# The context's expert rows in four parts of 64 tokens, rows of v of one part alternating with rows of u of the next

## The chip, the core and the metric

The kernel runs on one core of a Trainium2 chip. The metric is the device time of one launch in microseconds (us). The engines are TensorE (PE, whose weight loads the profile shows apart as PEld), VectorE (DVE), ScalarE (ACT), GpSimd (POOL), and SyncE (SP), which issues the plain loads. Every engine takes its instructions in a fixed order that was settled when the program was built; an instruction whose input is not there holds up all that stands behind it on its engine.

## The reference

Two layers over 256 latent tokens (`x`, 256x1024 float32) and 256 context tokens (`z`). The first layer updates both streams; the last one needs the context only for the scan's state. Per layer and stream:

```python
px = modulate(rmsnorm(x)) @ w_in          # columns: q,k,v | beta | alpha | gate | pool | fourier
x  = x + xg1 * mixer_out(px, scan(px))    # gated DeltaNet in chunks of 64, pooling, 2-D Fourier
hx = modulate(rmsnorm(x))
x  = x + xg2 * peer(hx)

def peer(h):                              # 8 heads, 16 of 128x128 experts each
    q = (h @ w_query).reshape(t, 8, 2, 128)
    s_top, i_top = top_k(q . sub_keys, 16)
    best, pos = top_k(s_top[0][:, None] + s_top[1][None], 16)
    idx, gate = i_top[0] * 128 + i_top[1], softmax(best)      # 128 choices per token
    act = gelu(einsum('td,tkd->tk', h, expert_u[idx]))
    return einsum('tk,tkd->td', gate * act, expert_v[idx])
```

A row of `expert_u` or `expert_v` is 1024 float32, 4 KB. A token needs 128 rows of each.

## The kernel before, in words

The program is written stage by stage for layer 0: the context's columns (the input projection with its convolutions), its scan and its update; the *context select* (`gather_select`: the choice of the 128 experts of each context token); then the latent columns, scan and update; the *latent select* (`dense_select`); `build`, which writes a dense table of gates to memory; and `stream`, which runs over all 128 slices of the expert tables for the latent tokens. Layer 1 follows in the same manner without a context select. A scheduler then moves instructions of later stages forward where their inputs and their buffers allow it, and fixes one order for each engine. So stages overlap, and what a stage may overlap with is set by engines, PSUM banks and SBUF space.

The latent tokens go through all experts (`stream`): in each of 128 iterations a slice of u and one of v (512 KB each) is loaded (L1100), split into a high part (ACT, L1106) and a low one (DVE, L1107), multiplied with the tokens (24 matmuls on PE, L1117 to L1119, into PSUM bank `s`), put through gelu (ACT, L1121), weighted (DVE, L1132, L1135; ACT, L1133) and multiplied with the slice of v (12 matmuls, L1140).

The context tokens fetch just their rows, by indirect DMAs of 128 rows that POOL issues (L970, `gather_rows`). Before the change the two halves of 128 tokens go by two ways.

- Tokens 0 to 127, *by choice*. For each of the 128 choices one gather brings a row of u for each token (`uv<-in_u`, 128x1024, 512 KB), and DVE multiplies it with the tokens and sums (L982, below "a dot"). Then, token by token, one gather brings the 128 rows of v that a token has chosen (`uv<-in_v`), and PE sums them with the weights (L1005; four matmuls for a pair of tokens, into bank `s`). There are seven buffers `uv`. All 256 of these gathers are written ahead of the stream (`EARLY = 256`), and the sums share bank `s` with the stream's scores.
- Tokens 128 to 255, *by token*. For each choice one gather brings u and v side by side (`uv<-in_uv`, 128x2048, 1 MB, from a table that holds both), DVE makes the dot (L1021), ACT gelu and gate (L1024, L1025), and DVE adds the weighted v to a sum (L1029). These 128 gathers are written inside the stream, ahead of the context's work for layer 1 (`context`), which needs their result.

In the context select DVE carries the searches for the largest scores (L772 to L780), the pairs (L825 to L866) and the index (L938); `oh` (L232) is a step of it on POOL, and the query projection (`po<-hT,w`, L256) runs on PE. In the latent columns `pj<-hT,w` and `pj<-w,hT` (L256) are the projections, `xpad` the padded input of the convolution, L495 and L497 the convolution on DVE. L632 opens the latent scan, whose steps `C` (L232) are on POOL, the queue of the gathers. L324 opens a normalization: that of `t` the columns, that of `xn` the latent select.

Of the kernel before, what the change touches and what calls it, by code (L numbers as in the profile page):

```python
# [95 lines left out]
def _layout(i):  # L96
# [25 lines left out]
    for l in range(depth):  # L122
# [9 lines left out]
        if l < depth - 1:  # L132
            a[f"u{l}"], a[f"v{l}"] = i["expert_u"][l], i["expert_v"][l]
            a[f"uv{l}"] = np.concatenate([i["expert_u"][l], i["expert_v"][l]], 1)
# [11 lines left out]
def _body(st, tc, a, out, dbg, until):  # L146
# [761 lines left out]

    def gather_select(l, s, m, rows, done):

        idx = rows("idx", [128, NB, HEADS * TOPK], 1, I32)
        idx_t = rows("idx_t", [128, T], 1, I32)
        gate = rows("gate", [128, NB, HEADS, TOPK])
        st = {}
        sc, sh = scales(l, 1, m, s)
        h2 = [normed(X[s, b], rows(f"h2{b}", [128, D]), f"n{b}") for b in range(NB)]
        done()
        sp = Stage("select")
        with using(c0="po", c1="po"):
            hT = transposed(h2, sc, sh, sp("hT", [128, KT, T]))  # L920

        def by_token():
            for b in range(NB):
                for half in range(2):
                    p = bank([128, 4, 128], f"c{half}")
                    for k in range(4):
                        pe.transpose(p[:, k], hT[:, half * 4 + k, b * 128 : b * 128 + 128], ident)
                    act.copy(h2[b][:, half * 512 : half * 512 + 512], p.rearrange("p a b -> p (a b)"))
# [5 lines left out]
        def after(h):  # L934
            if h == 0:
                by_token()
            for t in (idx, idx_f):
                dve.scalar_tensor_tensor(  # L938
                    t[:, :, h * TOPK : h * TOPK + TOPK], keys[0][:, :, 0], float(NKEYS), keys[0][:, :, 1],
                    op0=OP.mult, op1=OP.add,  # L940
                )

        keys = [None]
        idx_f = sp("idx_f", [128, NB, HEADS * TOPK])
        select(l, sp, (hT,), pair, lambda h, n: gate[:, :, h : h + n], GROUPS, after)

        p = bank([128, T], "c2")
        for b in range(NB):
            pe.transpose(p[:, b * 128 : b * 128 + 128], idx_f[:, b], ident)
        dve.tensor_copy(idx_t, p)  # L950
        for b in range(NB):
            st["h2", b], st["idx", b], st["gate", b] = h2[b], idx[:, b], gate[:, b]
            dump(f"idx{l}{s}{b}", st["idx", b])
            dump(f"gate{l}{s}{b}", st["gate", b])
        st["idx_t"] = idx_t
# [334 lines left out]
```

## Time and profile before

| what | us |
|---|---|
| median of three runs (3271.42 to 3287.86) | 3277.94 |
| the profiled execution, its own time | 3268.07 |
| its span, first to last instruction | 3266.3 |
| PE busy | 2874.7 (88%) |
| DVE busy | 2211.1 (68%) |
| ACT busy | 1349.3 (41%) |
| POOL busy | 860.3 (26%) |

What lies outside the span is 1.8 us. Busy shares are means over stages with different limits, so the table alone doesn't tell what a stage waits for; the rows further down are taken stage by stage. The gathers are the software queue in the profile: 268.46 MB of 746.52 MB in all.

### The profile page before, as it was taken

To read this page: it belongs to the slowest core of one execution; us is meant where nothing else is said; L and a number is where in the kernel's file an instruction comes from. 1 tells how busy PE (TensorE), PEld (TensorE's weight loads), DVE (VectorE), ACT (ScalarE), POOL (GpSimd) and SP (SyncE) were. 2 spreads that over 40 slices of the span, in tenths; PEclk is the share of its full clock that TensorE was granted. 3 is DMA by queue.
4 is the path that set the end of the run, shared out by engine and by line. 5 is a ranking of instruction groups with operands and counts; after the bars stand their busy time and mean duration, and the time that the engine had idled before them with its cause. 6 is when DMAs were issued, how large, how long until landed. Compare 5 with 4: busy or idle time off the path is not lost. (4 is left out here: it accounts for less than half of the span.)

```text
span 3266.3 us, 47152 instructions
## 1 busy us (share of the span) xinstructions
PE 2874.7 (88%) x17467; PEld 2362.5 (72%) x17467; DVE 2211.1 (68%) x4920; ACT 1349.3 (41%) x2352; POOL 860.3 (26%) x638
## 2 busy tenths in 40 slices
PE   7998985779796887887899999999779889999998
PEld 4686845637351776776778999867678778889997
DVE  4534979777880888898885655742599865555555
ACT  4432232101350444444455645542335644544443
POOL 0150148973545333333310123133320000000000
PEclk9998987779999999999899999999889999999999
DMA  7631466697999999999976543361335576666663
GB/s 260 207 103 54 138 244 194 201 330 254 354 373 351 375 369 365 362 395 387 360 278 197 161 140 118 94 221 43 100 123 176 205 237 202 200 210 202 213 212 130
DMA packets 246165, 746.52 MB, mean 229 GB/s; under 512 B 21168, under 2 KB 94256, under 8 KB 225456
## 3 DMA queue, kind: packets, MB, share of 16 engines
q1 hardware_dynamic: 190320, 474.54, 43.3%
q0 software_dynamic: 55296, 268.46, 22.1%
q8 instruction: 137, 2.24, 0.3%
q14 instruction: 92, 0.75, 0.1%
q10 hardware_dynamic: 320, 0.52, 0.1%
HBM read 707.27 MB, written 35.65 MB: 227 GB/s over the span
## 5 line engine op out<-in xcount | busy, mean ns | idle before, releaser
L1117 PE MATMUL s<-Hh,hu 128*128 128x256 f32 x2048 | 605.5, 296 | 75.7 <-ACT hu L1106 53.6
L1119 PE MATMUL s<-Hh,lu 128*128 128x256 f32 x2048 | 603.9, 295 | 55.5 <-DVE lu L1107 55.4
L1118 PE MATMUL s<-Hl,hu 128*128 128x256 f32 x2048 | 596.1, 291 | 0.0
L1117 PEld LDWEIGHTS s<-Hh,hu 128*128 128x128 f32 x2048 | 408.4, 199 | 100.8 <-ACT hu L1106 63.6
L1107 DVE TENSOR_TENSOR lu<-w,hu 128x1024 fp32r<-128x1024 f32 x256 | 317.0, 1238 | 225.4 <-ACT hu L1106 224.7
L1119 PEld LDWEIGHTS s<-Hh,lu 128*128 128x128 f32 x2048 | 408.8, 200 | 68.7 <-DVE lu L1107 68.6
L1107 DVE TENSOR_TENSOR lv<-w,hv 128x1024 fp32r<-128x1024 f32 x256 | 314.4, 1228 | 181.2 <-ACT hv L1106 168.1
L1118 PEld LDWEIGHTS s<-Hl,hu 128*128 128x128 f32 x2048 | 409.0, 200 | 7.8
L1106 ACT CAST hu<-w 128x1024 fp32r<-128x1024 f32 x256 | 267.8, 1046 | 328.3 <-PE s L1118 252.6
L1106 ACT CAST hv<-w 128x1024 fp32r<-128x1024 f32 x256 | 267.4, 1045 | 161.3 <-PE pj L1140 117.8
L970 POOL DMA_INDIRECT uv<-in_uv,idx x128 | 208.4, 1628 | 404.6 <-DVE acc L1029 383.4
L982 DVE SCALAR_TENSOR_TENSOR uv<-uv,h 128x1024 f32<-128x1024 f32 x128 | 193.4, 1528 | 38.7 <-DMA uv<-in_u,idx 37.8
L232 POOL TENSOR_TENSOR C<-L,levels 128x512 f32<-128x512 f32 x96 | 136.8, 1436 | 292.6 <-DMA g<-gd 161.1
L970 POOL DMA_INDIRECT uv<-in_u,idx x128 | 174.5, 1364 | 44.7 <-issue 25.2
L1140 PE MATMUL po<-hv,wh 128*128 128x512 f32 x512 | 164.9, 402 | 13.2 <-ACT wh L1133 12.2
L970 POOL DMA_INDIRECT uv<-in_v,idx_t x128 | 132.3, 1034 | 122.2 <-PE s L1005 95.2
L1140 PE MATMUL po<-lv,wh 128*128 128x512 f32 x512 | 162.4, 398 | 0.6 <-DVE lv L1107 0.5
L1029 DVE SCALAR_TENSOR_TENSOR acc<-uv,dot,acc 128x1024 f32<-128x1024 f32 x127 | 162.6, 1281 | 0.0
L1140 PE MATMUL pj<-hv,wh 128*128 128x512 f32 x512 | 162.5, 397 | 0.0
L1133 ACT CAST wh<-we 128x256 fp32r<-128x256 f32 x256 | 103.4, 404 | 143.0 <-DVE we L1132 78.3
L1088 PEld LDWEIGHTS c<-one,two 128*128 128x128 f32 x1024 | 123.6, 193 | 53.3 <-issue 33.2
L1140 PE MATMUL po<-hv,wl 128*128 128x512 f32 x512 | 161.8, 397 | 0.0
(427 smaller groups left out, 6007.5 us busy)
## 6 DMA issues: line engine op xcount, KB each, us to landing
w<-in_tab SPq DMA_DIRECT2D x512, 512.0 KB, 4.7
w<-in_wmod SPq DMA_DIRECT2D x96, 512.0 KB, 4.8
gd<-gs SPq DMA_DIRECT2D x32, 1024.0 KB, 5.3
g<-gd SPq DMA_DIRECT2D x32, 1024.0 KB, 8.5
w<-in_wq SPq DMA_DIRECT2D x48, 512.0 KB, 4.2
w<-in_win SPq DMA_DIRECT2D x44, 512.0 KB, 4.3
w<-in_wrest SPq DMA_DIRECT2D x24, 512.0 KB, 3.7
w<-in_wout SPq DMA_DIRECT2D x24, 512.0 KB, 5.3
```

The source lines that it names most:

```text
L232: pool.tensor_tensor(out, x, y, op=op)
L970: pool.indirect_dma_start(out=t, out_offset=None, in_=a[f"{table}{l}"], in_offset=bass.IndirectOffsetOnAxis(ap=index, axis=0))
L982: dve.scalar_tensor_tensor(u, u, 1.0, st["h2", b], op0=OP.mult, op1=OP.mult, accum_out=dots[:, j : j + 1])
L1029: dve.scalar_tensor_tensor(acc, uv[:, D:], dot, acc, op0=OP.mult, op1=OP.add)
L1088: pe.matmul(p[:, t], two[:, t], one[:, t], start=True, stop=True)
L1106: act.copy(hi, raw)
L1107: eng(lo, raw, hi.bitcast(F32), op=OP.subtract)
L1117: pe.matmul(p, hi[:, ks], Hh[:, k], start=(k == 0), stop=False)
L1118: pe.matmul(p, hi[:, ks], Hl[:, k], start=False, stop=False)
L1119: pe.matmul(p, lo[:, ks], Hh[:, k], start=False, stop=(k == KT - 1))
L1133: act.copy(wh, w)
L1140: pe.matmul(acc[b][n], x[:, ts], y[:, n * 512 : n * 512 + 512], start=(i == 0 and j == 0), stop=(i == NKEYS - 1 and j == 2),)
```

## The change

All 256 context tokens now go by choice, in four parts of 64 tokens. A gather of u holds two choices of the 64 tokens of a part (the lower half of the partitions one choice, the upper half the next), so a part needs 64 gathers of u, and 64 gathers of v, one for each token. `sums(i)`, the rows of v of part i, alternates with `scores(i + 1)`, the rows of u of the next part, one gather of each in turn. The table with u and v side by side and the way by token are gone, and with them L1024, L1025 and L1029. In all there are 512 gathers of 512 KB, where there were 256 of 512 KB and 128 of 1 MB: the same number of bytes.

The select now makes an index in the new layout for each head as soon as it is known: two small DVE instructions, eight small matmuls into bank `s`, a DVE copy. It also makes a copy of the tokens for each part (16 matmuls, two ACT copies) and takes the gates' softmax for all heads at the end. The buffers of the gathers (`uv`, `wz`, `h2`) now live in the stage `rows`, which is open from the context select on; before, `uv` and `wz` were opened after it. The sums of parts 0 and 1 use bank `s`, those of parts 2 and 3 bank `c2`. All gathers are written ahead of the stream.

```diff
-        h2 = [normed(X[s, b], rows(f"h2{b}", [128, D]), f"n{b}") for b in range(NB)]
+        h2 = [rows(f"h2{i}", [128, D]) for i in range(PARTS)]
...
         def after(h):
-            if h == 0:
-                by_token()
-            for t in (idx, idx_f):
-                dve.scalar_tensor_tensor(
...
+            if h < PARTS:
+                by_token(h)
+            js = slice(h * TOPK // 2, (h + 1) * TOPK // 2)
...
+                    pe.matmul(
+                        p[c * FEW : c * FEW + FEW, i], ident[:, o : o + FEW], idx_f[:, i * FEW // 128, c, js],
+                        start=True, stop=True,
+                    )
+            dve.tensor_copy(idx[:, :, js], p)
...
+        def scores(i):
+            dots = rows("dots", [128, FEW], 2)
+            for j in range(FEW):
+                u = fetch("u", st["idx"][:, i, j : j + 1])
+                dve.scalar_tensor_tensor(u, u, 1.0, st["h2"][i], op0=OP.mult, op1=OP.mult, accum_out=dots[:, j : j + 1])
+                yield
...
+        def sums(i):
+            dve.tensor_copy(spots_of, w_t[i].rearrange("p (g r) -> p g r", g=2))
+            p = bank([128, 512], VB[i])
+            for r in range(pairs):
+                vs = []
+                for g in range(2):
+                    t = i * FEW + g * pairs + r
+                    vs.append(fetch("v", st["idx_t"][:, t : t + 1]))
+                    yield
...
+        yield from scores(0)
+        for i in range(PARTS):
+            chains = [sums(i)] + ([scores(i + 1)] if i + 1 < PARTS else [])
+            while chains:
+                for c in list(chains):
+                    if next(c, c) is c:
+                        chains.remove(c)
+                    else:
                         yield
...
-    ROWS, EARLY = 7, 256
+    ROWS = 7
+    VB = ("s", "s", "c2", "c2")
...
-    fetching = gather_rows(0, CTX, m, rows, chosen)
-    for _ in range(EARLY):
-        next(fetching)
...
+    for _ in gather_rows(0, CTX, m, rows, chosen):
+        pass
```

The scheduler's order after the change differs in many places. Three of them follow; a number behind a name only tells buffers of one name apart.

On POOL, around the context select, before: the padding of the latent columns (`xpad`) stands ahead of the select's `oh`, and no gather stands between the `oh`.

```order
L232 TENSOR_TENSOR S_1992<-S_407_1946,dc_357 128x512
L482 MEMSET xpad_783_3490 128x2x2
L483 MEMSET xpad_783_3490 128x2x2
L482 MEMSET xpad_784_3491 128x2x2
L483 MEMSET xpad_784_3491 128x2x2
L232 TENSOR_TENSOR oh_2675<-oh_2675,tif_2626 128x1024
L232 TENSOR_TENSOR oh_2803<-oh_2803,tif_2754 128x1024
L232 TENSOR_TENSOR oh_2901<-oh_2901,tif_2852 128x1024
```

The same engine and place after: two `oh`, then 16 gathers of u, two `oh`, and so on; 55 gathers stand ahead of `xpad`, of which the last and the first two behind it are here.

```order
L984 DMA uv_7077<-in_u,idx_2452 128x1024
L481 MEMSET xpad_798_3624 128x2x2
L482 MEMSET xpad_798_3624 128x2x2
L481 MEMSET xpad_799_3625 128x2x2
L482 MEMSET xpad_799_3625 128x2x2
L984 DMA uv_7080<-in_u,idx_2452 128x1024
L984 DMA uv_7083<-in_u,idx_2452 128x1024
```

The latent columns have moved from ahead of the context select to behind it. Counted over POOL's order, ahead of the latent scan's `qd` (L232) there are 104 gathers after and 25 before; ahead of `Hl` (L232), in the latent select, 201 and 141; ahead of the last `oh` of the latent select 231 and 161.

On DVE, inside the context select, before: convolutions of the latent columns (L497) among the searches.

```order
L778 MAX best_2528<-rest_654_2965 128x8
L497 SCALAR_TENSOR_TENSOR y_3647<-xpad_783_3490,convw,y_3647 128x256
L780 MAX_INDEX pos_2963<-best_2528,rest_653_2964 128x8
L778 MAX tv_2949<-rest_646_2951 128x8
L857 TENSOR_TENSOR oh_2901<-ij_2896,places 128x1024
```

The same engine and stage after: dots (L993) among the searches.

```order
L993 SCALAR_TENSOR_TENSOR uv_6942,dots_6914<-uv_6942,h_526_2455 128x1024
L844 TENSOR_SCALAR start_2924<-row_2921 128x32
L849 CAST ij_2929<-row_2921 128x2x16
L777 MAX tv_2878<-rest_624_2880 128x8
L777 MAX tv_2878<-rest_625_2881 128x8
L993 SCALAR_TENSOR_TENSOR uv_6945,dots_6914<-uv_6945,h_526_2455 128x1024
L777 MAX tv_2878<-rest_626_2882 128x8
```

Between the first search and the copy of `idx_t` there are 48 convolution steps (L495, L497) and no dot before, and 48 dots and no convolution after. Up to the first instruction of the latent scan DVE has 15 dots before and 79 after; up to the stream 128 and 192.

On PE, inside the stream, before: the second products of an iteration (L1140) are followed by the first products of another (L1117).

```order
L1140 MATMUL po_7691<-hv_8440,wl_8447 128x512
L1140 MATMUL pj_1843_7692<-hv_8440,wl_8447 128x512
L1140 MATMUL pj_1844_7693<-hv_8440,wl_8447 128x512
L1117 MATMUL s_7694<-Hh_4947,hu_7857 128x256
L1118 MATMUL s_7694<-Hl_4948,hu_7857 128x256
```

The same after, where matmuls on rows of v (L1016) stand between them.

```order
L1138 MATMUL pj_2135_8786<-hv_9534,wl_9541 128x512
L1138 MATMUL pj_2136_8787<-hv_9534,wl_9541 128x512
L1016 MATMUL c_1926_8036<-uv_8085,wz_6912 32x512
L1016 MATMUL c_1926_8036<-uv_8080,wz_6912 32x512
L1016 MATMUL c_1926_8036<-uv_8085,wz_6912 32x512
L1115 MATMUL s_8788<-Hh_5081,hu_8951 128x256
L1116 MATMUL s_8788<-Hl_5082,hu_8951 128x256
```

Parts 2 and 3, 64 pairs of tokens or 256 such matmuls, stand inside the first 62 iterations of the stream, with 64 dots on DVE beside them. The 256 matmuls of parts 0 and 1 stand ahead of the stream, the first 100 of them ahead of the end of the latent scan.

## Rows read from the trace of the kernel before

**Rows 1.** Windows: busy (count) of PE, PEld, DVE, ACT, POOL; clock, DMA share, GB/s.
```profile
320.00:441.00 121.00, 111.42 (x531) 91.61 (x530) 112.20 (x611) 32.92 (x79) 17.58 (x9) 0.99 0.43 129
441.00:486.00 45.00, 39.57 (x152) 24.37 (x150) 29.27 (x65) 10.99 (x28) 28.70 (x25) 0.84 0.88 331
486.00:736.00 250.00, 173.79 (x865) 127.14 (x865) 209.89 (x307) 45.91 (x107) 214.01 (x157) 0.76 0.73 243
736.00:866.00 130.00, 111.11 (x596) 72.31 (x596) 108.01 (x584) 27.47 (x47) 53.27 (x43) 0.96 0.81 286
866.00:1052.00 186.00, 156.61 (x879) 72.66 (x880) 96.94 (x284) 63.85 (x67) 90.66 (x87) 0.98 0.98 372
1052.00:1673.00 621.00, 514.88 (x2933) 447.19 (x2931) 542.32 (x709) 271.02 (x582) 208.45 (x128) 0.93 0.97 368
1673.00:2045.00 372.00, 370.64 (x2450) 335.67 (x2451) 219.25 (x335) 206.21 (x324) 59.29 (x47) 1.00 0.50 162
```

**Rows 2.** Timelines, landmarks: start us, us, engine line op names [idle before].
```profile
319.94 0.87 DVE L772 MAX8 tv<-sco 128x8 f32<-128x128 f32 x4 [3.56 <-ACT sco L805]
...
763.65 0.87 DVE L772 MAX8 tv<-sco 128x8 f32<-128x128 f32 x4 [14.55 <-ACT sco L805]
...
848.58 0.22 DVE L866 TENSOR_TENSOR sel<-oh 128x64 f32<-128x64 bf16 x1
```

**Rows 3.** DVE in the context select: groups (count, busy us, mean ns, idle before), first row.
```profile
L497 DVE SCALAR_TENSOR_TENSOR y<-xpad,convw,y 128x256 f32<-128x256 f32 x36 | 15.9, 478 | 0.0
```

**Rows 4.** Two lines over the whole trace: ns min/median/max, first and last start.
```profile
L324 ACT ACTIVATE t<-x x6: 1039/1056/1059, 6.3 to 2047.7; 128x1024 f32<-128x1024 f32 x6
L324 ACT ACTIVATE h<-x x2: 1039/1048/1057, 293.2 to 295.3; 128x1024 f32<-128x1024 f32 x2
...
L632 DVE TENSOR_TENSOR L<-c,mask_l x10: 676/684/692, 142.6 to 2166.2; 128x512 f32<-128x512 f32 x10
```

**Rows 5.** DVE between 486 and 736 us, groups; the dots.
```profile
L982 DVE SCALAR_TENSOR_TENSOR uv<-uv,h 128x1024 f32<-128x1024 f32 x109 | 170.4, 1581 | 30.9 <-DMA uv<-in_u,idx 30.1
```

**Rows 6.** POOL between 486 and 736 us, groups.
```profile
L970 POOL DMA_INDIRECT uv<-in_u,idx x104 | 147.6, 1420 | 29.0 <-issue 20.8 <-DVE uv L982 5.0 <-PE c L667 0.6
L232 POOL TENSOR_TENSOR C<-L,levels 128x512 f32<-128x512 f32 x24 | 32.2, 1348 | 0.4
```

**Rows 7.** POOL in the latent scan, timeline.
```profile
564.55 1.78 POOL L970 DMA_INDIRECT uv<-in_u,idx  x1 [0.16 <-issue]
566.63 0.94 POOL L970 DMA_INDIRECT uv<-in_u,idx  x1 [0.30 <-DVE uv L982]
```

**Rows 8.** Instructions on `uv` over the whole trace: ns min/median/max, first and last start.
```profile
L970 POOL DMA_INDIRECT uv<-in_v,idx_t x128: 932/938/2458, 722.8 to 1042.6; - x128
```

**Rows 9.** Waits between 980 and 1060 us: us in total, times, longest.
```profile
PEld s L1005 <- DMA uv<-in_v,idx_t: 63.6, 45, 2.8
DVE upd L904 <- DMA h<-sum: 63.0, 1, 63.0
```

**Rows 10.** Matmuls on rows of v, window: busy us (records) of PE and PEld.
```profile
950.00:1000.00 50.00, 26.48 (x112) 3.64 (x106) 0.97 1.00 377
```

**Rows 11.** Stream beside the gathers, 1052 to 1673 us, groups.
```profile
L970 POOL DMA_INDIRECT uv<-in_uv,idx x128 | 208.4, 1628 | 404.6 <-DVE acc L1029 383.4 <-DVE upd L904 10.7 <-DVE uv L1021 5.7
...
L1021 DVE SCALAR_TENSOR_TENSOR uv<-uv,h 128x1024 f32<-128x1024 f32 x128 | 156.3, 1221 | 5.3 <-DMA uv<-in_uv,idx 5.3
...
L1107 DVE TENSOR_TENSOR lu<-w,hu 128x1024 fp32r<-128x1024 f32 x81 | 99.1, 1224 | 51.3 <-ACT hu L1106 51.3
```

**Rows 12.** Rest of that stream, 1673 to 2045 us, groups, first row.
```profile
L1117 PE MATMUL s<-Hh,hu 128*128 128x256 f32 x367 | 107.7, 293 | 0.6 <-ACT we L1121 0.6
```

**Rows 13.** Layer 1's stream, 2900 to 3200 us, groups.
```profile
L1107 DVE TENSOR_TENSOR lu<-w,hu 128x1024 fp32r<-128x1024 f32 x53 | 65.0, 1226 | 62.9 <-ACT hu L1106 62.9
```

**Rows 14.** The fastest 50 us of DMA in the stream.
```profile
1450.00:1500.00 50.00, 41.50 (x244) 35.94 (x243) 45.58 (x60) 22.14 (x49) 18.27 (x11) 0.93 1.02 398
```

**Rows 15.** DMA issues: count, KB each, us to landing.
```profile
w<-in_tab SPq DMA_DIRECT2D x512, 512.0 KB, 4.7
```

More of the change, by code (lines that the diff above doesn't have):

```diff
@@ L947, in gather_select @@
-        p = bank([128, T], "c2")
+        idx_f = sp("idx_f", [128, NB, 2, HEADS * TOPK // 2])
+        gate = sp("gate", [128, NB, HEADS, TOPK])
+        select(l, sp, (hT,), pair, lambda h, n: gate[:, :, h : h + n], (HEADS,), after)
+        gate_c = sp("gate_c", [128, NB, 2, HEADS * TOPK // 2])
         for b in range(NB):
[L949 to L954, printed above, removed]
@@ L1033, in gather_rows @@
-        make = Stage("by_choice")
-        yield from by_choice(make, 0)
-        make.close()
-        make = Stage("by_token")
-        acc = yield from by_token(make, 1)
-        make.close()
-        halves = [[t[:, n * 512 : n * 512 + 512] for n in range(2)] for t in (st["h2", 0], acc)]
-        residual(l, s, m, halves)
+        def scores(i):
[4 more added lines that the diff above has]
+                yield
+            p = bank([128, FEW], VB[i])
+            for c in range(2):
+                cs = slice(c * FEW, c * FEW + FEW)
+                pe.matmul(p[cs], dots, ident[:, cs], start=True, stop=True)
+            w = w_t[i] = rows("w_t", [128, FEW], 2)
+            act.activation(w, p, AF.Gelu)
+            dve.tensor_tensor(w, w, st["gate_t"][:, i * FEW : i * FEW + FEW], OP.mult)
@@ new lines, in sums @@
+        def sums(i):
[7 more added lines that the diff above has]
+                    yield
+                for n in range(2):
+                    for g in range(2):
+                        o = 32 * (2 * n + g)
+                        pe.matmul(
+                            p[o : o + 32], wz[:, g * pairs + r], vs[g][:, n * 512 : n * 512 + 512],
+                            start=(r == 0), stop=(r == pairs - 1), tile_position=(0, o),
+                        )
+            out = rows("uv", [128, D], ROWS)[:, 0:512]
+            act.copy(out, p)
+            b, o = divmod(i * FEW, 128)
+            for n in range(2):
+                act.dma_start(
+                    st["h2"][2 * b][o : o + FEW, n * 512 : n * 512 + 512], out[n * FEW : n * FEW + FEW]
+                )
@@ L1206, in _body @@
         modulation(1, (1, 0))
+    for _ in gather_rows(0, CTX, m, rows, chosen):
+        pass
     def context():
-        for _ in fetching:
-            pass
         rows.close()
```

115 lines of the change are left out of this document (38 added, 77 removed).

## The prediction

> **What bounds the kernel now.** I read the stages in windows first [rows 1], then the landmarks that part them [rows 2, 4], then each stage's groups and waits. The windows show four kinds of stage. In the context select (320 to 441 us) DVE is busy 112.2 of 121 us, PE 111.4, and POOL hardly at all; 48 convolution steps of the latent columns run inside it, 36 of them L497 [rows 3], so that only 45 us lie between its end and the first instruction of the latent scan at 486. In the latent scan and update (486 to 736) POOL is busy 214 us and idle between gathers for another 29 [rows 6]: gathers and the scan's steps `C` take turns on one queue [rows 7], and this queue sets the pace, though DVE has 210 us of work too. In the latent select (736 to 866) DVE leads with 108 of 130. From 866 to 1052 the DMA queues are full (0.98, 372 GB/s). At the end of it DVE stands still for 63 us before the residual's first update [rows 9], because the stream can start only when the sums have left bank `s`.
>
> The stream then has two parts. Beside the wide gathers (1052 to 1673) it makes 81 iterations [rows 11] in 621 us, 7.67 us each, with DVE at 542 us and the DMA queues at 0.97. After them PE is busy 370.6 of 372 us. An iteration that PE alone bounds takes 300 / 53 = 5.66 us [rows 13]. The rest of that stretch has 367 / 8 = 46 iterations [rows 12], 260 us, so the context's work for layer 1 costs PE some 110 us of it.
>
> **The change part by part.**
>
> A. *The context select.* Eight heads of a select that carries neither gathers' dots nor another stage's convolutions take 848.8 - 763.7 = 85 us [rows 2]. The 48 dots that the order puts into the context select come on top, on the engine that leads. A dot takes 1.22 us by itself [rows 11] and 1.58 + 0.08 beside POOL's issuing [rows 5]; I take 1.5, since gathers are issued beside these too: 72 us. The index copies, eight short ones, add 2. From 320 that makes 479 instead of 441: +38. With 1.22 the end is 464; with 1.66 and a wait for the landing of 30.1 / 109 = 0.28 us for each [rows 5] it is about 498.
>
> B. *The latent columns.* Today they are hidden behind the select but for 45 us. In the new order their normalization, transposes, projections and convolutions all stand behind the copy of `idx_t`; the buffers of the gathers are now held from the select on, and I take that to be the reason, which no row shows. Their whole length is paid. The nearest stages are layer 1's latent columns, 2166.2 - 2047.7 = 118 us from normalization to scan, and the context's, 142.6 - 6.3 = 136 us [rows 4]. Both split their operands and need three products where the layer 0 latent columns need one, but have no dots beside them, where this stage has 31. I take 112, close to the nearer one, with 95 and 136 as the ends. The scan then starts at 479 + 112 = 591 instead of 486: **+105**, between 464 + 95 - 486 = +73 and 498 + 136 - 486 = +148. This is the term on which the forecast rests.
>
> C. *Latent scan and update.* Between `qd` and `Hl` POOL issues 201 - 104 = 97 gathers instead of 141 - 25 = 116. With 1.42 us and 29.0 / 111 = 0.26 idle for each [rows 6], 19 fewer are worth 19 x 1.68 = 32 us. DVE has 59 dots here instead of 113, so it leaves the pace to POOL for certain; and a gather's issue takes between 0.93 and 1.78 us [rows 7, 8], the short one where no dot runs, so the rest gets cheaper as well. On the other side 25 pairs of rows of v now stand in PE's order among the steps of the scan, and each can wait for its landing. I take **-40**. At best all gathers take 0.94 + 0.26 and the other 58 us of POOL's work stay (214 less 147.6 for u and 8 for v): 97 x 1.20 + 58 = 174 instead of 250, -76; a context scan and update without gathers took 293.2 - 142.6 = 151 us [rows 4], so that isn't out of reach. At worst the waits on v eat most of the gain: -10.
>
> D. *Latent select.* Thirty gathers instead of twenty stand ahead of its last `oh`, with some ten dots on the leading engine: 10 x 1.3 = 13 us, part of it in the 14.6 us that DVE waits for the first scores [rows 2]. I take **+8** (0 to +25).
>
> E. *From there to the stream.* Gathers up to the last row of part 1: 320 - 231 = 89, instead of 95. The stretch is bound by them and by the DMA queues, so it stays near 186 us; fewer pairs of v on PE (22 instead of some 43) free buffers sooner. I take **-5**. If the gathers were no bound, DVE's 96.9 us [rows 1] and 46 dots at 1.3 would be: 157 us, -29; at worst +5.
>
> F. *The stream of layer 0.* What goes: 128 dots, 128 weighted sums and the small gelus in lockstep with them, two instructions of 1.2 to 1.3 us in each step on DVE. What comes: 64 dots on DVE, and 64 pairs of rows of v on PE. A pair costs 26.48 us for 112 records, eight to a pair: 1.9 us [rows 10]; with a little waiting I take 2.0. The 62 iterations that carry them need 62 x 5.66 + 64 x 2.0 = 479 us of PE. DMA needs for the same 192 gathers of 0.524 MB and 62 iterations of two loads of 512 KB [rows 15] and 0.13 MB of gates, 174 MB, which at the 368 GB/s of the stretch before [rows 1] is 473 us. Two resources that both need all of the time don't overlap perfectly; I take 495. The other 66 iterations at 5.66 and the context's 110 give 484. Together 979 against 621 + 372 = 993, -14; the residual's four updates now stand only two iterations behind the last sum, which may cost DVE, and the low halves `lu` behind it, 4. So **-10**. At best DMA runs at 398 GB/s [rows 14] and the matmuls of a pair hide half their time: about -50. At worst PE waits for each pair as it did ahead of the stream, 63.6 us in 45 waits [rows 9]: 64 waits of 1.4 are 90, less what the buffers cover, +35.
>
> *On the size of the gathers.* The wide gathers, 1 MB each, run with the loads at 368 GB/s, and the 512 KB ones with 377 [rows 1, 10]: no loss for the smaller size shows. The Trainium skill (DMA: Bandwidth & Descriptors, section "Measured (HBM→SBUF, 128 partitions, SWDGE, issued from GpSimd)") advises to batch transfers to 1 MiB or more, and the section on the anatomy of a DMA gives some 2.0 us of fixed cost for each; by that, as an estimate, 192 gathers at 3.2 us in a row would need 614 us and make the stream 120 us longer. This trace disagrees, since gathers overlap, and F stands as it is.
>
> G. *The rest*, layer 1, isn't touched. The latent columns of layer 1 wait for the end of the stream, so a shift there goes to the end in full.
>
> The sum: +105 - 40 + 8 - 5 - 10 = +58. The profiled execution took 3268.07 us (its span and 1.8 us around it), so 3326 by that execution; the median of the runs shown is 9.9 us above it, and I state 3335.
>
> **The rivals.**
>
> 1. *The gathers were the brake, and fewer of them per stage give the shift back.* C and E at their best with the rest as forecast: 105 - 76 + 8 - 29 - 10 = -2, 3276, no change. For it: POOL's 1.78 against 0.94 us. Against: both need that every wait for a row of v is hidden, in stages whose order puts PE and POOL in turn.
>
> 2. *The other side: the stream gains as well.* Its mechanism is the lockstep between DVE's dots, ACT's gelus and the low halves `lu` at 7.67 us an iteration: with the wide dots gone, PE alone sets the pace. It is priced at F's best, -50, and with rival 1 gives -42, 3236. With the rest as forecast it makes the kernel faster by more than 16 us once the scan starts less than 71 us late (71 - 40 + 8 - 5 - 50 = -16); at 105 late it needs rival 1 as well. For it: DVE's 542 of 621 us. Against: PE gets 128 us of new work just there, and DMA's need is the same.
>
> 3. *PE pays for the rows of v.* All of C's gain is lost and F is at its worst: 105 - 10 + 8 + 35 = +138, 3416. For it: PE waited in 45 places for 63.6 us ahead of the stream. Against: there the DMA queues were full, in the scan they are at 0.73.
>
> 4. *The overlap isn't lost.* If the latent columns start earlier than their place in the order makes it seem, B shrinks to the 45 us it costs today, the scan starts 38 us late and the sum is -9, 3269. Against: an engine doesn't pass over an instruction, and on DVE, PE and POOL alike the columns stand behind the select.
>
> **How the numbers follow.** The forecast has 0.65, rival 1 0.12, rival 2 0.07, rival 3 0.13, rival 4 0.03. The forecast's own range is 3295 to 3380. Two in ten may be left out: 3270 to 3400 leaves rival 2 and the far end of rival 3. About 0.5%, 16 us, is what a measurement of this kernel can tell from no change. Slower than that: the forecast almost whole and rival 3, 0.77; no change: rivals 1 and 4 in the main, 0.13; faster: rival 2 and a part of rival 1, 0.10.
>
> **What would show it.** A and B: the last search of the context select ends between 464 and 498 us, the first L631 comes near 591, and no convolution starts before the select's end. C: POOL's gathers between `qd` and `Hl` average under 1.42 us, and L324 of the latent select comes some 65 us later than 736. E and F: the first matmul of the stream near 1110, 62 iterations of about 8 us with PE busier than now, then 5.7 us. Wrong it would be if the convolutions ran inside the select, or if the scan took under 180 us, or if the stream's first 62 iterations came near 7 us.

## The result, and where the time went

The changed kernel takes 3407.31 us, the median of 4 runs (3403.23 to 3412.97), beside 3274.68 us for the kernel before (median of 4). The ratio is 1.0404, with a 95% interval of 1.0361 to 1.0447: 4% slower, above the forecast of 3335 us and 7 us above its range of 3270 to 3400. The direction was as forecast. Of the mechanism, the lost cover of the latent columns was; the largest single loss, 64 more gathers ahead of the stream, was not. The shift between the two profiled spans is 3402.5 - 3266.3 = 136.2 us, where the sum had 58.

The windows of the changed kernel, from landmark to landmark (columns as in [rows 1]; the edges are the landmarks of the table below):

```profile
312.20:478.00 165.80, 83.43 (x519) 68.41 (x518) 145.65 (x617) 15.66 (x34) 72.80 (x56) 0.73 0.57 197
478.00:621.00 143.00, 119.58 (x516) 73.63 (x516) 78.74 (x218) 35.20 (x86) 64.82 (x60) 0.89 0.80 280
621.00:841.00 220.00, 189.17 (x1054) 112.11 (x1054) 119.25 (x181) 44.78 (x107) 163.41 (x136) 0.93 0.71 235
841.00:978.80 137.80, 98.72 (x483) 65.40 (x480) 120.73 (x576) 22.07 (x41) 63.35 (x48) 0.85 0.81 281
978.80:1177.90 199.10, 141.70 (x714) 77.05 (x714) 164.57 (x421) 71.99 (x72) 106.26 (x93) 0.84 0.97 352
1177.90:1685.60 507.70, 503.45 (x2780) 339.62 (x2781) 270.58 (x382) 170.01 (x256) 218.24 (x189) 0.99 0.94 338
1685.60:2177.60 492.00, 489.88 (x3226) 442.23 (x3225) 283.72 (x413) 255.59 (x398) 61.41 (x46) 1.00 0.54 168
```

The same windows with the gathers alone (us, POOL busy and count, clock, DMA share, GB/s):

```profile
312.20:478.00 165.80, 57.42 (x48) 0.73 0.57 197
478.00:621.00 143.00, 62.24 (x55) 0.89 0.80 280
621.00:841.00 220.00, 107.00 (x90) 0.93 0.71 235
841.00:978.80 137.80, 43.31 (x39) 0.85 0.81 281
978.80:1177.90 199.10, 106.26 (x93) 0.84 0.97 352
1177.90:1685.60 507.70, 218.24 (x189) 0.99 0.94 338
```

The landmarks in the changed kernel (one line each: ns min/median/max, first and last start, as in [rows 4]); `pair` ends the context select, `sel` the latent one:

```profile
L865 DVE TENSOR_TENSOR pair<-oh x8: 205/220/225, 328.5 to 478.0; 128x64 f32<-128x64 bf16 x8
L865 DVE TENSOR_TENSOR sel<-oh x8: 200/211/227, 922.3 to 978.8; 128x64 f32<-128x64 bf16 x8
```

```profile
L631 DVE TENSOR_TENSOR L<-c,mask_l x2: 682/687/692, 621.0 to 624.6; 128x512 f32<-128x512 f32 x2
```

```profile
L323 ACT ACTIVATE xn<-x x2: 1055/1056/1058, 841.0 to 842.5; 128x1024 f32<-128x1024 f32 x2
```

```profile
L1115 PE MATMUL s<-Hh,hu x2048: 277/283/583, 1177.9 to 3380.4; 128*128 128x256 f32 x187
```

```profile
L903 DVE TENSOR_TENSOR upd<-po,row x2: 692/692/692, 2177.6 to 2180.7; 128x512 f32<-128x512 f32 x2
```

The same landmarks in the kernel before:

```profile
L866 DVE TENSOR_TENSOR pair<-oh x8: 211/220/224, 333.5 to 440.0; 128x64 f32<-128x64 bf16 x8
L632 DVE TENSOR_TENSOR L<-c,mask_l x2: 680/686/691, 486.2 to 492.6; 128x512 f32<-128x512 f32 x2
L324 ACT ACTIVATE xn<-x x2: 1056/1056/1057, 736.5 to 737.9; 128x1024 f32<-128x1024 f32 x2
L1117 PE MATMUL s<-Hh,hu x369: 278/283/582, 1050.6 to 1398.6; 128*128 128x256 f32 x185
L904 DVE TENSOR_TENSOR upd<-po,row x2: 692/692/692, 2040.1 to 2043.2; 128x512 f32<-128x512 f32 x2
```

The latent select of the kernel before ends at 848.6 [rows 2].

| term | landmark | before | after | forecast | measured |
|---|---|---|---|---|---|
| A | last pair of the context select | 440.0 | 478.0 | +38 | +38.0 |
| A and B | first instruction of the latent scan (L632, now L631) | 486.2 | 621.0 | +105 | +134.8 |
| C | scan and update, up to the normalization of `xn` | 250.3 | 220.0 | -40 | -30.3 |
| D | latent select, up to its last `sel` | 112.1 | 137.8 | +8 | +25.7 |
| E | from there to the stream's first matmul | 202.0 | 199.1 | -5 | -2.9 |
| F | stream of layer 0, up to the latent residual | 989.5 | 999.7 | -10 | +10.2 |
| G | the rest | 1226.2 | 1224.9 | 0 | -1.3 |

What the reader is to see: only the scan and update got clearly shorter, by 30 us, and each of the other stages that took dots or rows of v in is longer where the engine that leads it is the one that these need. In the context select DVE has 146 us of work instead of 112 [rows 1]. PE, which the columns no longer fill there, has 83 of 166 us, and its granted clock falls from 0.99 to 0.73 in that window. In the columns, which now stand alone, PE leads with 120 of 143 us; in the latent select DVE with 121 of 138; in the stream beside the gathers PE with 503 of 508. Ahead of the stream 48 + 55 + 90 + 39 + 93 = 325 gathers are made, where the kernel before made 25 + 111 + 28 + 94 = 258 up to that point.

### The profile page after: what moved, and what is told of

The parts are those of the page before. It is cut to its first block, busy times and chain, and to the rows that moved or that the text cites. A ratio compares the mean times of both kernels' runs of the same rounds, so it can differ in the third digit from the quotient of the medians.

```text
span 3402.5 us, 48547 instructions
## 1 busy us (share of the span) xinstructions
PE 3010.3 (88%) x18236; PEld 2356.4 (69%) x18236; DVE 2070.2 (61%) x4798; ACT 1302.7 (38%) x2104; POOL 937.0 (28%) x766
## 5 line engine op out<-in xcount | busy, mean ns | idle before, releaser
L1117 PE MATMUL s<-Hh,lu 128*128 128x256 f32 x2048 | 588.5, 287 | 4.6 <-DVE lu L1105 4.6
L993 DVE SCALAR_TENSOR_TENSOR uv<-uv,h 128x1024 f32<-128x1024 f32 x256 | 336.1, 1317 | 149.1 <-DMA uv<-in_u,idx 127.9
L1117 PEld LDWEIGHTS s<-Hh,lu 128*128 128x128 f32 x2048 | 396.4, 194 | 28.9 <-issue 17.8
L1116 PEld LDWEIGHTS s<-Hl,hu 128*128 128x128 f32 x2048 | 396.3, 194 | 8.3 <-issue 1.7
L984 POOL DMA_INDIRECT uv<-in_v,idx_t x256 | 292.0, 1141 | 345.4 <-PE c L1016 172.2
L984 POOL DMA_INDIRECT uv<-in_u,idx x256 | 302.5, 1182 | 233.0 <-DVE uv L993 78.7
L1130 DVE TENSOR_TENSOR we<-we,g 128x256 f32<-128x256 f32 x256 | 116.6, 465 | 205.4 <-ACT we L1119 186.7
L1119 ACT ACTIVATE we<-s 128x256 f32<-128x256 f32 x256 | 97.4, 380 | 292.2 <-PE s L1117 289.9
L1016 PE MATMUL s<-uv,wz 128*32 128x512 f32 x512 | 142.8, 691 | 56.2 <-DMA uv<-in_v,idx_t 56.1
L1086 PEld LDWEIGHTS c<-one,two 128*128 128x128 f32 x1024 | 129.2, 195 | 78.2 <-issue 35.5
L1086 PE MATMUL c<-one,two 128*128 128x128 f32 x1024 | 146.1, 290 | 39.8 <-DVE one L1085 37.5
L1138 PE MATMUL pj<-hv,wl 128*128 128x512 f32 x512 | 163.4, 398 | 0.0
```

The costliest lines, as they stand in the source:

```text
L984: pool.indirect_dma_start(out=t, out_offset=None, in_=a[f"{table}{l}"], in_offset=bass.IndirectOffsetOnAxis(ap=index, axis=0))
L993: dve.scalar_tensor_tensor(u, u, 1.0, st["h2"][i], op0=OP.mult, op1=OP.mult, accum_out=dots[:, j : j + 1])
L1016: pe.matmul(p[o : o + 32], wz[:, g * pairs + r], vs[g][:, n * 512 : n * 512 + 512], start=(r == 0), stop=(r == pairs - 1), tile_position=( ...
L1086: pe.matmul(p[:, t], two[:, t], one[:, t], start=True, stop=True)
L1116: pe.matmul(p, hi[:, ks], Hl[:, k], start=False, stop=False)
L1117: pe.matmul(p, lo[:, ks], Hh[:, k], start=False, stop=(k == KT - 1))
```

## The experiments

Theory 1: the lost cover of the latent columns is the loss, and only the place of the buffers took it away. Theory 2: the alternation of v and u costs it wherever the columns stand. After the first four runs theory 3 was added: 64 gathers more have to be made ahead of the stream. All ratios are to the kernel before.

**wz_late.** One buffer, 8 KB of each partition, is opened later:

```diff
-        wz = rows("wz", [128, FEW, pairs])
+        late = Stage("late")
+        wz = late("wz", [128, FEW, pairs])
...
+        late.close()
```

The stage `late` opens when the stages of the select are closed.

> One line of the changed kernel: the 8 KB (per partition) of wz lie in a stage of their own that opens after the select, instead of in the stage that is held from the select on. In the order of instructions the latent columns' convolutions then stand inside the context select again, the 48 early dots stay there too. Theory 1 (the loss is the lost cover of the latent columns, and only the place of the buffers took it away): the first scan instruction comes near 525 us instead of 621 (select to about 480, then the 45 us that the columns cost before), and the kernel takes 3300 to 3340 us. Theory 2 (the alternation of v and u itself costs it, the columns are only where it shows): the scan starts earlier, but the gathers take it back, 3385 or more.

Measured: 3362.65 us, 1.0251 (1.0229 to 1.0274). The scan starts at 545.8 us, 75 earlier, with the convolutions inside the select. But only some 45 us of it arrive at the end: 41 between the profiled spans, 45 between the medians, 1.5% or 50 us between the two ratios. Theory 1 has the sign and less than half of the size; theory 2's 3385 and more did not come. Where the rest went is seen in the gathers of the stretch ahead of the stream:

```profile
907.70:1148.50 240.80, 141.60 (x125) 0.78 0.98 359
```

This stretch now has 125 gathers to make instead of 93, at 1.93 us each, and is 42 us longer.

**before_held.** The other way round: the kernel before, with unused space below the select.

```diff
+    hs = Stage("held")
+    pool.memset(hs("held", [128, 10496])[:, 0:8], 0.0)
     cw = Stage("select_weights")
...
     cw.close()
+    hs.close()
```

> The kernel before, with 41 KB per partition held unused under the context select and released right after it, so that the select's tiles lie where they lie in the changed kernel. Nothing of the gathers is changed in the program (the order lets them begin a little earlier). Theory 1 (place of the buffers): the convolutions of the latent columns move behind the select, the scan starts 70 to 140 us late, 560 to 625, and the kernel takes 3340 to 3390 us. Theory 2 (the alternation): within 20 us of the kernel before, 3255 to 3295.

Measured: 3313.94 us, 1.0111 (1.0084 to 1.0138), with the scan at 617.9. So 41 KB of unused space cost 1.1%. The program's gathers are the same, but the order now lets 61 of them be issued in the select, where the kernel before has none. That the place of the buffers uncovers the columns is shown: no convolution is left in the select, and the columns take 138 us. The size lies between the two expectations, because the gathers went on meanwhile. Their windows from the select's end, for the columns, the scan and update, the latent select and the stretch up to the stream:

```profile
479.70:617.90 138.20, 88.64 (x75) 0.90 0.98 371
617.90:838.50 220.60, 83.16 (x87) 0.98 0.69 231
838.50:957.10 118.60, 26.87 (x28) 0.91 0.71 246
957.10:1000.20 43.10, 8.73 (x8) 1.00 0.82 290
```

With all but 8 gathers made by the end of the latent select, the stream follows after 43 us, not 202. It even starts 50 us earlier than in the kernel before (1000.2 against 1050.6) and is 87 us longer (1076.5 against 989.5). A part of that is only moved: of the 512 matmuls of `build`, all ahead of the stream's first matmul in the kernel before, 371 stand behind it here.

```profile
L1088 PE MATMUL c<-one,two 128*128 128x128 f32 x371 | 53.2, 291 | 12.4 <-ACT gs L1089 10.8 <-DVE one L1087 1.7
```

So the first matmul of the stream is not the same point of the work in every run. From the end of the latent select to the end of the stream the two take 1119.6 and 1191.5 us: of 108 us that the select ends later, 72 are won back.

**own_stage.** All buffers of the gathers open after the select, as in the kernel before.

```diff
-        wz = rows("wz", [128, FEW, pairs])
+        make = Stage("gathers")
+        wz = make("wz", [128, FEW, pairs])
...
-            t = rows("uv", [128, D], ROWS)
+            t = make("uv", [128, D], ROWS)
...
+        make.close()
```

The small buffers `dots` and `w_t` move in the same way.

> The changed kernel with all buffers of the gathers (uv, wz, dots, w_t) in a stage of their own that opens after the select, as in the kernel before. No dot is left in the select, and the columns are covered again. Theory 1: the scan starts near 490 us; the 48 gathers that were made in the select come later, on a path that POOL and the DMA queues set, at some 1.4 us each (67 us) at most; 3270 to 3340 us. Theory 2: 3385 or more.

Measured: 3393.08 us, 1.0346 (1.0321 to 1.0371), in the range that was written down for theory 2. Theory 1 falls as the whole cause: the scan starts at 495.0 and the latent select ends at 884.5, 94 us earlier than in the changed kernel, and the stream starts 8 us later, because the gathers are late:

```profile
884.50:1185.90 301.40, 185.68 (x161) 0.73 0.95 353
```

**short_dots.** Each dot over 128 of 1024 columns.

```diff
-                dve.scalar_tensor_tensor(u, u, 1.0, st["h2"][i], ...
+                dve.scalar_tensor_tensor(u[:, 0:128], u[:, 0:128], 1.0, st["h2"][i][:, 0:128], ...
```

> The changed kernel, each dot over 128 of its 1024 columns only (this leaves out seven eighths of the scores' sums); gathers, matmuls and places of the buffers are the same. If the dots on DVE set the length of the select and of the columns: the select ends near 445 instead of 478, the columns take about 112 us instead of 143, the scan starts near 555, and the kernel takes 3320 to 3350 us. If the landing of the gathers and a slow PE clock made the columns long: they stay at 135 or more, and only the select gains, 3360 to 3385.

Measured: 3276.27 us, 0.9989 (0.9973 to 1.0005): the dots' time on DVE is worth as much as the whole loss, and more than either case of the expectation gave it. It is no share of the loss, since the kernel before makes 256 dots as well. The first reading was right for the select (it ends at 438.6) and wrong for the columns, which stay at 138.1 us; ACT's steps under the next run tell why. The other gains: scan and update 203.6, latent select 117.1, stretch ahead of the stream 162.3.

**no_rows.** No gathers, dots or sums; their space stays held (edit: the loop of `gather_rows` is left out, and an unused buffer of 37 KB takes the place of its buffers).

> The changed kernel without the gathers, the dots, the sums of rows of v and their small steps (the residual adds what stands in the buffers); the buffers' space stays held, so the latent columns stay uncovered. It measures the stages by themselves. If the columns are long by themselves, from the end of the select to the first scan instruction it takes 130 to 143 us; if the gathers beside them make them long, about 112. The select ends near 400. The stream without gathers takes 835 to 870 us. 2900 to 2960 us in all.

Measured: 2951.78 us in one run. The stages by themselves: context select 107.9 us (314.0 to 421.9), columns 110.5, scan and update 149.1, latent select 111.0. From its first matmul the stream takes 940.8 us, more than I expected, with PE almost full:

```profile
421.90:532.40 110.50, 101.42 (x446) 70.08 (x446) 38.35 (x149) 33.85 (x84) 2.55 (x5) 0.94 0.35 109
...
788.90:1729.70 940.80, 916.40 (x5997) 826.61 (x5997) 591.89 (x993) 490.71 (x717) 62.58 (x46) 0.99 0.55 186
```

The 940.8 us are not the stream alone. The 512 matmuls of `build`, which the changed kernel runs ahead of its stream, stand inside it here:

```profile
L1077 PE MATMUL c<-one,two 128*128 128x128 f32 x512 | 70.1, 281 | 14.4 <-DVE one L1076 8.8 <-ACT gs L1078 5.6
```

In the changed kernel all 512 (L1086, 80.1 us of PE) lie between 978.8 and 1177.9 us. Without them the stream would take some 856 us (940.8 - 70.1 - 14.4, an estimate), as expected.

The columns are lengthened from 110.5 to 143.0 us by what the gathers bring. Where, ACT's own steps tell (timeline: start us, us). First the changed kernel, then the one without gathers, then short_dots; L323 opens the normalization, the last L340 ends the transposes, L490 is the copy of a projection:

```profile
481.84 1.06 ACT L323 ACTIVATE t<-x 128x1024 f32<-128x1024 f32 x1 [8.47 <-PE c L968]
508.13 0.56 ACT L340 ACTIVATE hT<-c,mod,sc 128x256 f32<-128x256 f32 x1 [3.50 <-DVE hT L342]
557.17 0.59 ACT L490 COPY xpad<-pj 128x512 f32<-128x512 f32 x1 [2.32 <-PE pj L255]
```

```profile
425.75 1.06 ACT L323 ACTIVATE t<-x 128x1024 f32<-128x1024 f32 x1 [7.07 <-PE c L970]
440.34 0.56 ACT L340 ACTIVATE hT<-c,mod,sc 128x256 f32<-128x256 f32 x1 [2.76 <-DVE hT L342]
487.57 0.59 ACT L490 COPY xpad<-pj 128x512 f32<-128x512 f32 x1 [3.01 <-PE pj L255]
```

```profile
442.57 1.06 ACT L323 ACTIVATE t<-x 128x1024 f32<-128x1024 f32 x1 [7.37 <-PE c L968]
461.15 0.57 ACT L340 ACTIVATE hT<-c,mod,sc 128x256 f32<-128x256 f32 x1 [3.07 <-DVE hT L342]
519.49 0.59 ACT L490 COPY xpad<-pj 128x512 f32<-128x512 f32 x1 [3.54 <-PE pj L255]
```

From L323 to the last L340 it is 26.3 us against 14.6; to the sixth L490 49.0 against 47.2; from there to the scan 63.8 against 44.8. The first 12 us are the normalization's small steps on DVE, which stand in its queue behind dots. Most of it is the dots' own time: with short dots this part takes 18.6 us, so 7.7 of the 11.7 go with them; the 4 that stay are not taken apart, dots still wait for their rows in them. Of the last 19, 14.7 are on PE, where the rows of v begin at 560 us: 66 records of matmuls on them. In short_dots the columns stay long because what the dots leave free is taken by rows of v: 96 records, 19.9 us, already ahead of the sixth L490 (58.3 us from the last L340, then 57.2 to the scan). A slow clock, the other half of that expectation, does not explain the last 19: TensorE's granted clock was 0.97 there, and 0.55 only in the first 30 us, where PE has 13 us of work. These two rows of the changed kernel are the wait between 478 and 621 us (us, times, longest) and, in a window of that time, L1016:

```profile
DVE uv L993 <- DMA uv<-in_u,idx: 35.9, 15, 6.2
```

```profile
478.00:621.00 143.00, 14.72 (x66) 0.89 0.80 280
```

**in_turn.** The changed kernel, one pair of chains undone:

```diff
-            chains = [sums(i)] + ([scores(i + 1)] if i + 1 < PARTS else [])
+            if i == PARTS // 2:
+                yield from scores(i)
+            chains = [sums(i)] + ([scores(i + 1)] if i + 1 in (1, 3) else [])
```

> The changed kernel with one pair of chains undone: the rows of v of the second part no longer alternate with the rows of u of the third, which are fetched after them. So 256 gathers, as in the kernel before, and not 320 have to be made ahead of the stream's first matmul; the buffers lie as in the changed kernel and the latent columns stay uncovered. Theory 3 (the 64 gathers more ahead of the stream, at some 2 us each, are the loss): the latent select ends near 979 as in the changed kernel, with 232 of 256 gathers made; the stream begins near 1030 instead of 1178, lasts 1000 to 1045 us, and the kernel takes 3250 to 3300 us. Theory 1 (the lost cover of the columns sets the start of the stream): the stream starts as late as before this edit, and it takes 3385 or more.

Measured: 3341.76 us, 1.0204 (1.0183 to 1.0225): half of the loss goes with this one edit, though the scan starts at 617.7, as late as in the changed kernel. Theory 3 holds, with a smaller size than expected (3250 to 3300); theory 1's 3385 and more did not come. The gathers' windows from the end of the latent select:

```profile
956.00:1065.80 109.80, 49.18 (x45) 0.97 0.96 369
1065.80:1741.60 675.80, 313.74 (x252) 0.96 0.95 344
```

The stream starts 112 us earlier, 20 of them gained in the latent select. But the 64 gathers with their dots are made in it now, with 64 of the 512 matmuls of `build` (8.6 us), and it takes 1054.2 us instead of 999.7. So a gather of u with its dot costs some 112 / 64 = 1.75 us ahead of the stream, and (54.5 - 8.6) / 64 = 0.7 us inside it.

**in_turn_wz.** Both edits.

> Both edits: 256 gathers ahead of the stream, and wz in a stage that opens after the select, so that the columns are covered. Theory 3: the latent select ends near 908 with some 200 gathers made, the 55 that are left take about 1.9 us each, the stream starts near 1013; 3235 to 3285 us, only some 15 less than with the first edit alone. If the cover and the gathers were two independent losses: 45 less than the first edit alone.

Measured: 3289.11 us, 1.0044 (1.0029 to 1.0060). With wz_late and in_turn it makes a table of four corners: the later wz is worth 1.5% with 320 gathers ahead of the stream (4.04 to 2.51) and 1.6% with 256 (2.04 to 0.44); the 64 gathers are worth 2.0% and 2.1%. My expectation that the second edit would add only 15 us was wrong: the two losses add up.

**turn_wz_c2.** Only the first part's sums in bank `s`.

```diff
-    VB = ("s", "s", "c2", "c2")
+    VB = ("s", "c2", "c2", "c2")
```

This stands on top of both edits above.

> As the run with both edits, and the sums of the second part in bank c2 instead of s, so that only the first part's 128 gathers must be made ahead of the stream. If the gathers left after the latent select are what keeps the stream waiting, it starts near 950, 43 us behind the select, and the kernel takes 3190 to 3260 us. If the stream is then bound by the DMA queues, or if c2 is needed by others ahead of it, nothing is gained on the run with both edits.

Measured: 3335.28 us, 1.0180 (1.0162 to 1.0198). The stream starts at 902.6, 140 us earlier than with both edits, and all of it is lost in the stream: beside 317 gathers it runs with DMA at 0.91 and PE busy 835 us for 914 us, and the kernel is 46 us slower. All 512 matmuls of `build` (68.7 us of PE) stand inside the stream here, so a part of the 140 us is only moved. What bounds this stream is not shown.

**own_turn.** own_stage with the edit of in_turn.

> The changed kernel with all buffers of the gathers in a stage that opens after the select, and with 256 gathers ahead of the stream: what is left of the change against the kernel before is the second half's rows (64 pairs of rows of v on PE in the stream instead of 128 wide gathers summed on DVE). If gathers made early, in the select, are worth what they cost there: some 110 are left after the latent select instead of 61, the stream starts near 1080 and the kernel takes 3310 to 3345 us, 20 to 55 more than with covered columns and early gathers (3289). If a dot in the select costs as much as its gather gives back later: 3275 to 3300.

Measured: 3332.12 us, 1.0182 (1.0155 to 1.0209), as expected if early gathers are worth their dots. It leaves 98 gathers for the stretch ahead of the stream, in_turn_wz 61. Against the kernel before, its profiled execution is 62 us longer, in the main 28 in the latent select (140.5 against 112.1 us, with 25 dots where the kernel before has none) and 34 in the stream (1023.4 against 989.5). The gathers ahead of the stream:

```profile
875.40:1080.00 204.60, 106.22 (x98) 0.92 0.95 357
```

**late_idx.** No gather in the context select (edit: the index of the dots is written once, after the last head).

> The changed kernel, the index of the dots written once after the last head instead of after each, so that no gather and no dot starts in the context select; buffers as in the changed kernel, columns uncovered. The select ends near 425 instead of 478, the columns take 125 to 145, the scan starts near 560. If gathers ahead of the stream set its start, 48 fewer made early cost what the select gains: the stream starts within 25 us of 1178 and the kernel takes 3385 to 3425. If the latent chain sets it: 3345 to 3370.

Measured: 3378.77 us, 1.0312 (1.0280 to 1.0343): neither case. The select ends at 416.8, 61 us earlier than in the changed kernel; 122 gathers are left at the end of the latent select instead of 93, and the stream starts 24.5 us earlier. With the columns uncovered, early dots cost more than they give; with covered columns (own_turn against in_turn_wz) it is the other way.

**short_v.** The matmuls of rows of v in the last two parts over 64 columns.

```diff
+                W = 64 if i > 1 and r > 0 else 512
...
-                            p[o : o + 32], wz[:, g * pairs + r], vs[g][:, n * 512 : n * 512 + 512],
+                            p[o : o + 32, 0:W], wz[:, g * pairs + r], vs[g][:, n * 512 : n * 512 + W],
```

> The changed kernel, the matmuls of the rows of v in the third and fourth part over 64 columns instead of 512, but for the first of each part (this leaves out most of these sums). If the stream beside the gathers is bound by PE alone, the kernel is about 90 to 100 us faster, 64 pairs at some 1.6 us less, 3300 to 3325. If the DMA queues take over at their 370 GB/s, the stretch of 508 us shortens to about 470 and the kernel takes 3360 to 3380.

Measured: 3359.59 us, 1.0253 (1.0223 to 1.0282): the DMA queues take over.

```profile
1177.60:1658.50 480.90, 435.58 (x2818) 359.04 (x2819) 274.38 (x387) 173.65 (x260) 222.90 (x189) 0.94 0.97 360
```

PE has 68 us less in this stretch, which shortens by 27.

**before_early.** What the runs point to: the kernel before, its gathers by choice begun in the select, wz alone opened late.

```diff
-            wz = make("wz", [128, half, pairs])
+            late = Stage("late")
+            wz = late("wz", [128, half, pairs])
...
-        make = Stage("by_choice")
-        yield from by_choice(make, 0)
-        make.close()
+        yield from by_choice(early, 0)
+        early.close()
...
     rows = Stage("rows")
+    early = Stage("early")
```

The stage `early` holds the other buffers of `by_choice`.

> The kernel before, its gathers begun early: the buffers of the gathers by choice lie below the select's and are held from it on, wz alone opens after it, so that the columns stay covered. If early gathers bring the stream forward and the stream keeps its length: the select ends near 525, the latent select near 900 with 200 of 256 gathers made, the stream starts 15 to 40 us earlier than in the kernel before, 3235 to 3265 us. If a dot in the select costs as much as its gather gives back: 3265 to 3300.

Measured: 3257.67 us (10 runs), 0.9955 (0.9937 to 0.9972): faster than the kernel before by 0.45%, 16 us, a small gain whose interval leaves out no change. In the profiled execution the stream starts at 1036.9 instead of 1050.6 and is about as long as before, 993.6 us against 989.5:

```profile
894.10:1036.90 142.80, 62.94 (x57) 0.97 0.98 375
```

## Why the prediction was too low

The step of the prediction that failed by the most is B, the latent columns: +134.8 us where it had +105. C, D and F were mis-sized to the same side, and the gathers that must be made ahead of the stream, to whose larger number E gave no price, are the largest loss that a single edit takes back.

A chain of runs leads from the kernel before to the changed one: the second half by choice and in alternation, own_turn, +1.8%; gathers begun in the select, in_turn_wz, -1.4; the columns uncovered, in_turn, +1.6; 64 more gathers ahead of the stream, the changed kernel, +2.0. The forecast rested on the third, took the second for a loss (A), and priced the fourth and what the first brought near nothing. From own_turn on there is one edit between two runs. The first step is many changes at once, and no run takes them apart; its 62 us are known by stage only.

- **A** came out at 478 as forecast, 479, by luck, from three terms that were off. The select begins at 312 us, not at 320; alone it takes 108 us (no_rows), not 85; a dot in it takes 1.25 us, not 1.5 (59.88 us of DVE for 48 dots and their read-outs). The 1.5 came from a wrong reading of [rows 5]: the dots there are long beside the scan's `C` on POOL and not beside gathers. By the timeline of the kernel before between 486 and 736 us, 63 dots that overlap a gather's issue but no `C` take 1.22 us on average, the 45 beside a `C` 2.1. One of each, with POOL's instruction beside it:

```profile
562.78 2.70 DVE L982 SCALAR_TENSOR_TENSOR uv<-uv,h 128x1024 f32<-128x1024 f32 x1
563.12 1.27 POOL L232 TENSOR_TENSOR C<-L,levels 128x512 f32<-128x512 f32 x1
570.49 1.21 DVE L982 SCALAR_TENSOR_TENSOR uv<-uv,h 128x1024 f32<-128x1024 f32 x1
571.11 1.41 POOL L970 DMA_INDIRECT uv<-in_u,idx  x1 [0.30 <-issue]
```

- **B** is the step that failed by the most, 30 us. The cause, the place of the buffers, was right and is shown by wz_late and before_held. The 112 us were right for the columns alone, 110.5. What lay beside them was put at nothing: I counted 31 dots there and gave them no time, though they hold up DVE's small steps (12 us, 8 of them the dots' own time), and forgot the rows of v, which need PE, the engine that leads this stage (14.7 of the last 19 us). The second part of the step failed too, "their whole length is paid": of 75 us that wz_late wins back at the scan, some 45 arrive.
- **C**, -30 for -40. POOL's issues got cheaper as forecast, 107.00 / 90 = 1.19 us against 1.42 [rows 6], and rows of v took 48 us of PE in this stage. By the timelines an issue that no dot overlaps takes 0.94 us in the kernel before and 0.96 in the changed one, one beside a dot 1.46 and 1.43; half of the 90 have no dot beside them, where it was 12 of 111.
- **D** was mis-sized by 18 us. I expected ten dots, a part of them under a wait; there were 18 in the leading engine's stage, 25 us. In in_turn, where one remains, the latent select takes 117.5 us. Two rows of the changed kernel's latent select: the dots (DVE busy, records with the read-outs), and ACT's wait behind `oh`, 10.5 us in the kernel before and 10.7 in in_turn. That `oh` is late because it stands behind gathers in POOL's queue fits the order; no run shows it by itself.

```profile
841.00:979.00 138.00, 25.32 (x36) 0.85 0.81 281
```

```profile
ACT tif L818 <- POOL oh L231: 43.7, 5, 11.6
```

- **E** was right in its number, -2.9, and hid the largest cause. "89 gathers instead of 95" holds only because the latent chain came so late that 64 more had been made by then. So B and E were not two terms to be priced apart: a chain that comes earlier finds more gathers left (125 in wz_late). What is left of B's gain after that adds to what 64 gathers fewer give, by the four corners.
- **F**, +10 for -10. The pair of rows of v costs what I took, 129.1 us of PE for 64 pairs, 2.0 each:

```profile
L1016 PE MATMUL c<-uv,wz 128*32 128x512 f32 x512 | 129.1, 605 | 0.0
```

  The stretch took 508 us where I had 495, with PE full, and the rest 492 where I had 484. The residual did not stall.
- **The rivals.** Rival 3's total of 3416 is the nearest, but not its mechanism: in the stream PE did not wait 1.4 us for each pair of rows of v (no idle time before L1016), it worked; C's gain was not lost. Rivals 1 and 4 are excluded by C and by the scan's start, and rival 2's stream needs both PE and DMA to have room, which short_v shows they have not.
- **The range.** Four terms of the sum erred to the same side. I read one cause in them, gather work put into stages whose leading engine it needs: shown for D (in_turn) and for the columns (no_rows, short_dots), argued for C and F from PE's busy time. So their errors add up; I had set the range as if they would partly cancel.

On the size of the gathers: beside 189 gathers of 512 KB the DMA queues moved 360 GB/s once PE gave way (short_v), against 368 with 128 of 1 MB [rows 1], 2% less. No run changes the size alone, and the other loads of the two stretches differ, so this bounds a loss by size and does not show one. The Trainium skill (DMA: Bandwidth & Descriptors, section "Measured (HBM→SBUF, 128 partitions, SWDGE, issued from GpSimd)") advises to batch transfers to 1 MiB or more; the trace here shows at most these 2% for half of that.

## What to carry to other kernels

Price moved work by the engine that leads the stage into which it goes, and count what must be finished ahead of a stage that waits (here 320 gathers instead of 256) before the landmarks in between. Terms that share a cause err together. When a chain comes earlier, a queue that ends at the same landmark has done less by then: of 75 us gained at the scan (wz_late) 29 reached the stream's first matmul. And before two runs are compared from landmark to landmark, look whether the same work stands between them: `build` moved across the stream's first matmul in four of the runs, in whole or in part. Before a buffer is held across a stage, look at what the scheduler can still move into that stage: 8 KB decided some 1.5% here.

## What I had not expected

- Space alone moves time: 41 KB held and never used, 1.1% slower (before_held).
- In the changed kernel's stream the gathers are nearly hidden and the rows of v are not. Without any gather it would take some 856 us (no_rows less `build`, an estimate), with 189 gathers and 64 pairs of rows of v it takes 999.7: 144 more, of which 129 are PE's matmuls on the rows of v. The 64 gathers more of in_turn cost some 0.7 us each in its stream; ahead of the stream a gather costs 1.75 to 1.93 us.
- The granted clock of TensorE differs in the context select: 0.99 before, with PE busy 111 of 121 us [rows 1], and 0.73, a mix of its two levels of 1.2 and 2.4 GHz, after, with PE busy 83 of 166 us.
